# Reading one MLP weight through six access patterns in a two-layer trunk

## The chip, the cores and the metric

The kernel runs on one core of one Trainium2 chip. The metric is the device time of the program in microseconds, the median over runs. The engines are named as in the profile: PE (TensorE, matmul), PEld (its loads of the stationary operand), DVE (VectorE), ACT (ScalarE), POOL (GpSimd) and SP (SyncE, which issues the DMAs).

## The reference

A trunk of two layers over 256 tokens of width 2048, in float32. The first layer's mixer is a gated linear recurrence (HGRN2), the second one's is gated linear attention (GLA). Each mixer is followed by an MLP with a squared ReLU, and each of these four parts has a norm before it, a norm behind it and a residual add:

```python
def sqrelu_mlp(h, w_up, w_down):
    u = jax.nn.relu(h @ w_up)
    return (u * u) @ w_down

    for i in range(DEPTH):
        hn = rmsnorm(h, norm_mix_pre[i])
        m = ...    # hgrn2_mixer(hn, ...) for i = 0, gla_mixer(hn, ...) for i = 1
        h = h + rmsnorm(m, norm_mix_post[i])
        f = sqrelu_mlp(rmsnorm(h, norm_mlp_pre[i]), mlp_w_up[i], mlp_w_down[i])
        h = h + rmsnorm(f, norm_mlp_post[i])
```

`mlp_w_up[i]` is 2048 x 8192, `mlp_w_down[i]` is 8192 x 2048. The change concerns `mlp_w_down[0]`.

## The kernel before

All weights are read once, in chunks of 1 MB, 128 partitions x 2048 float32. `load_chunk` (L90) takes one of three `raw` buffers and issues the DMA on SP. `split` (L97) makes two reduced-precision parts out of each half of a chunk, 128 x 1024: `hi` by a copy on ACT (L101) and `lo` as the difference on DVE (L102), into five buffers each. The activations are held in two parts in the same way (class `Xhl`), transposed, with the contracted dimension on the partitions. A product is then three matmuls instead of one full-precision one: hi x hi, hi x lo and lo x hi.

Two forms of product follow. `gemm` (L120) has a token tile (128 tokens) of the activations as the stationary operand and 512 weight columns as the moving one; its chunks hold 4 k-tiles of 128 rows with 512 columns each, laid out by `_rows` on the host. `mm_half` (L110) issues the matmuls of half a chunk for one token tile: two k-tiles, three matmuls each (L116, L117, L118). `gemmT` (L129) has 128 weight columns as the stationary operand and the tokens as the moving one (L136 with 512 columns, both parts; L137 with 256).

The MLP goes over its 8192 hidden features in 8 groups of 1024. `up(g)` computes a group's features with 8 `gemmT` calls (in group 0 the first four column tiles come from the stage before), and `down(g)` multiplies them by the group's 1024 rows of the second weight, in 4 column blocks of 512. The running sums are kept in SBUF and added to on DVE (L443). The order is `up(0)`, then `up(g)` and `down(g - 1)` for g = 1 to 7, then `down(7)` with three column blocks; the last column block of group 7 belongs to `transition`, which also does the norms and the start of the next part. `transition` has a hand-written order; elsewhere a scheduler sets the order on each engine from the code and its buffers.

The scores of the mixers (`scores`) are products in full float32, 128 columns for each head. For `s` in `LEVELS` the moving operand is read through a pattern of its own, `comb(1, s)`: runs of `s` elements, in turn from two places 1024 + s elements apart, and so on along the tile. The products before and after the loop read contiguously.

## Time and profile before

| | |
|---|---|
| median time (two runs) | 2360.14 us (2359.75 to 2360.53) |
| span of the profiled execution, first to last instruction | 2358.0 us |
| mean granted TensorE clock | 0.997 |
| PE busy | 2328.4 us, 99% |
| DVE busy | 1499.1 us, 64% |
| ACT busy | 1193.5 us, 51% |
| DMA | 433.61 MB, 184 GB/s over the span |
| matmuls of `mm_half` (L116 to L118) | 3 x 1856, 392 ns mean duration |
| matmuls of `gemmT` (L136, L137) | 2 x 2704, 397 and 282 ns mean duration |

The profile gives the span of its execution; the median of the timed runs, 2360.14 us, is 2.1 us above it. [...] Shares of the span are averages over stages; the change is read from the stage that it lies in, the first layer's MLP, from about 540 to 1220 us.

### The profile page before, as it was taken

How to read it: one execution, taken by the hardware profiler on the slowest of the kernel's cores; microseconds unless marked ns; L12 is line 12 of the kernel's file. 1: busy time of each engine (PE TensorE's matmuls, PEld its weight loads, DVE VectorE, ACT ScalarE, POOL GpSimd, SP SyncE). 2: the span in 40 equal slices, each digit the busy share in tenths (PEclk: the TensorE clock that was granted, in tenths of full speed). 3: DMA queues.
4: the chain of work that ended last, by engine and by line, in shares of the span. 5: the costliest groups of instructions: out<-in, count | busy, mean ns of one | idle time of the engine just before them, and what ended most of it. 6: DMA issues, size and time to landing. Idle time of an engine off the chain costs nothing.

```text
span 2358.0 us, 29704 instructions
## 1 busy us (share of the span) xinstructions
PE 2328.4 (99%) x11784; PEld 1970.0 (84%) x11784; DVE 1499.1 (64%) x2047; ACT 1193.5 (51%) x1738; POOL 46.4 (2%) x22
## 2 busy tenths in 40 slices
PE   8999999999999999999989999999999999999998
PEld 7888888878888888888878888887888888888887
DVE  6787776666565565565576667656656566566556
ACT  7454554456454454454447446554645445445443
POOL 0000000020000000000010000002000000000000
PEclk9999999999999999999999999999999999999999
DMA  8545445545555555555554645454555555555554
GB/s 315 169 158 172 166 159 176 174 157 206 185 194 188 188 194 185 192 189 188 194 168 154 213 144 171 167 184 158 202 191 194 185 193 188 189 195 183 192 196 139
DMA packets 65867, 433.61 MB, mean 184 GB/s; under 512 B 7968, under 2 KB 8352, under 8 KB 15168
## 3 DMA queue, kind: packets, MB, share of 16 engines
q1 hardware_dynamic: 65728, 431.71, 53.6%
q8 instruction: 92, 1.51, 0.3%
q14 instruction: 47, 0.39, 0.0%
HBM read 429.59 MB, written 2.10 MB: 183 GB/s over the span
## 4 chain that ended last, share of the span: by engine, by line
PE 96%; DVE 3%; ACT 0%; DMA 0%; SPq 0%; issue 0%; DVEq 0%; ACTq 0%
PE mmT L136 27%; PE mm L118 17%; PE mm L117 17%; PE mm L116 17%; PE mmT L137 14%; PE sc L502 2%; DVE h L300 2%; PE tr L171 1%; DVE xhl L184 1%; PE po L563 0%; PE po L566 0%; PE po L565 0%; DMA raw<-w_hin 0%; DVE tok L279 0%; ACT xhl L182 0%; PE pg L698 0%
## 5 line engine op out<-in xcount | busy, mean ns | idle before, releaser
L102 DVE TENSOR_TENSOR lo<-raw,hi 128x1024 fp32r<-128x1024 f32 x776 | 948.7, 1225 | 734.7 <-ACT hi L101 733.6
L101 ACT ACTIVATE hi<-raw 128x1024 fp32r<-128x1024 f32 x794 | 839.6, 1061 | 997.7 <-PE mm L118 595.4
L136 PE MATMUL mmT<-xhl,hi 128*128 128x512 f32 x2704 | 954.3, 397 | 0.1
L137 PE MATMUL mmT<-xhl,lo 128*128 128x256 f32 x2704 | 761.2, 282 | 0.8 <-DVE lo L102 0.8
L116 PE MATMUL mm<-hi,xhl 128*128 128x512 f32 x1856 | 728.3, 394 | 6.0 <-ACT hi L234 6.0
L118 PE MATMUL mm<-hi,xhl 128*128 128x512 f32 x1856 | 725.2, 391 | 7.4 <-DVE xhl L184 7.4
L117 PE MATMUL mm<-lo,xhl 128*128 128x512 f32 x1856 | 726.7, 392 | 0.5 <-DVE lo L235 0.5
L136 PEld LDWEIGHTS mmT<-xhl,hi 128*128 128x128 f32 x2704 | 507.5, 188 | 122.3 <-issue 1.0
L137 PEld LDWEIGHTS mmT<-xhl,lo 128*128 128x128 f32 x2704 | 510.8, 189 | 3.4 <-issue 1.3
L118 PEld LDWEIGHTS mm<-hi,xhl 128*128 128x128 f32 x1856 | 349.6, 188 | 82.1 <-DVE xhl L184 9.2
L116 PEld LDWEIGHTS mm<-hi,xhl 128*128 128x128 f32 x1856 | 349.4, 188 | 77.8 <-ACT hi L234 7.2
L117 PEld LDWEIGHTS mm<-lo,xhl 128*128 128x128 f32 x1856 | 349.8, 188 | 72.6 <-DVE lo L235 1.4
L102 POOL TENSOR_TENSOR lo<-raw,hi 128x1024 fp32r<-128x1024 f32 x18 | 46.2, 2574 | 1603.2 <-ACT hi L101 1592.7
L145 DVE TENSOR_TENSOR half<-mmT,half 128x256 f32<-128x256 f32 x169 | 70.5, 418 | 0.0
L443 DVE TENSOR_TENSOR tok<-tok,mm 128x512 f32<-128x512 f32 x108 | 69.0, 680 | 0.0
L144 ACT COPY half<-mmT 128x256 f32<-128x256 f32 x169 | 59.6, 353 | 0.0
L429 DVE SCALAR_TENSOR_TENSOR half<-half,rr 128x256 f32<-128x256 f32 x120 | 51.1, 425 | 4.2
L432 ACT ACTIVATE half<-half 128x256 f32<-128x256 f32 x120 | 50.3, 420 | 3.7
L433 DVE TENSOR_TENSOR xhl<-half,xhl 128x256 fp32r<-128x256 f32 x120 | 50.2, 418 | 0.0
L300 DVE SCALAR_TENSOR_TENSOR h<-tok,col,h 128x512 f32<-128x512 f32 x32 | 48.5, 1553 | 0.3
L502 PEld LDWEIGHTS sc<-qk,kc 128*128 128x128 f32 x336 | 46.2, 191 | 2.8
L431 ACT ACTIVATE xhl<-half 128x256 fp32r<-128x256 f32 x120 | 48.0, 400 | 0.0
(125 smaller groups left out, 764.3 us busy)
## 6 DMA issues: line engine op xcount, KB each, us to landing
raw<-w_up SPq DMA_DIRECT2D x128, 1024.0 KB, 4.8
raw<-w_dn SPq DMA_DIRECT2D x128, 1024.0 KB, 4.8
raw<-w_hin SPq DMA_DIRECT2D x58, 1024.0 KB, 4.8
raw<-w_gin SPq DMA_DIRECT2D x48, 1024.0 KB, 4.8
raw<-w_hout SPq DMA_DIRECT2D x16, 1024.0 KB, 4.8
raw<-w_gout SPq DMA_DIRECT2D x16, 1024.0 KB, 4.8
raw<-w_hin SPq DMA_DIRECT2D x11, 512.0 KB, 7.2
wp<-npost SPq DMA_DIRECT2D x16, 256.0 KB, 3.3
```

The lines of the kernel that those rows point to most:

```text
L101: A.activation(hi, raw, AF.Copy)
L102: (eng or V).tensor_tensor(lo, raw, hi.bitcast(F32), ALU.subtract)
L116: PE.matmul(ps, xh, hi[:, kk, :], start=(k == 0), stop=False)
L117: PE.matmul(ps, xh, lo[:, kk, :], start=False, stop=False)
L118: PE.matmul(ps, xl, hi[:, kk, :], start=False, stop=(k == nk - 1))
L136: PE.matmul(ps, hi[:, kk * P:(kk + 1) * P], X.both(k), start=(k == 0), stop=False)
L137: PE.matmul(ps[:, 0, :], lo[:, kk * P:(kk + 1) * P], X.both(k)[:, 0, :], start=False, stop=(k == KT - 1))
L144: A.copy(u, ps[:, 1, :])
L145: V.tensor_tensor(u, ps[:, 0, :], u, ALU.add)
L300: V.scalar_tensor_tensor(hs, self.mw[n, t], self.r[t], hs, ALU.mult, ALU.add)
L443: V.tensor_tensor(m[n, t], m[n, t], ps[t], ALU.add)
L502: PE.matmul(ps[:, hd, :], l(hd * kt + k), r(hd * kt + k), start=(k == 0), stop=(k == kt - 1))
```

## The change

`ORDERS` holds an entry for each of the 8 groups of the hidden features: none for groups 0 and 7, and an offset and a list of [step, count] pairs (outermost first, in elements) for groups 1 to 6. On the host, `_ordered` permutes the columns inside each block of 512 of `mlp_w_down[0]`, for these groups and for the first three of the four column blocks: column j goes to the place that the pattern reaches as its j-th. In the kernel, `mm_half` reads the 512 columns of `hi` and `lo` through the pattern, so that the matmul gets them in the old order. The patterns are: 1, the even places and then the odd ones; 2, pairs of neighbours in turn from the lower and the upper half; 3, runs of 16 in turn from the two halves; 4, runs of 8 likewise; 5, backwards; 6, four runs of 128, the last one first. Everything else, the last column block and the second layer included, stays. The build with the new code issues the same instructions in the same order on every engine.

```diff
+ORDERS = (None,
+          (0, [[1, 2], [2, 256]]),
+          (0, [[2, 128], [256, 2], [1, 2]]),
+          (0, [[16, 16], [256, 2], [1, 16]]),
+          (0, [[8, 32], [256, 2], [1, 8]]),
+          (511, [[-1, 512]]),
+          (384, [[-128, 4], [1, 128]]),
+          None)
...
-    def mm_half(ps, half, hf, xs, t, nk):
+    def mm_half(ps, half, hf, xs, t, nk, order=None):
         hi, lo = (w.rearrange("p (k n) -> p k n", k=2) for w in half)
+
+        def cols(w):
+            if order is None:
+                return w
+            off, steps = order
+            return bass.AP(tensor=w.tensor, offset=w.offset + off,
+                           ap=[list(w.ap[0])] + [list(s) for s in steps])
+
         for kk in range(2):
             k = 2 * hf + kk
             xh, xl = xs(k, t)
-            PE.matmul(ps, xh, hi[:, kk, :], start=(k == 0), stop=False)
-            PE.matmul(ps, xh, lo[:, kk, :], start=False, stop=False)
-            PE.matmul(ps, xl, hi[:, kk, :], start=False, stop=(k == nk - 1))
+            PE.matmul(ps, xh, cols(hi[:, kk, :]), start=(k == 0), stop=False)
+            PE.matmul(ps, xh, cols(lo[:, kk, :]), start=False, stop=False)
+            PE.matmul(ps, xl, cols(hi[:, kk, :]), start=False, stop=(k == nk - 1))
...
-    def gemm(wap, base, nk, xs):
+    def gemm(wap, base, nk, xs, order=None):
...
-                    mm_half(ps[t], half, 2 * c + j, xs, t, nk)
+                    mm_half(ps[t], half, 2 * c + j, xs, t, nk, order)
...
         def down(g):
             for n in range(4 if g < NG - 1 else 3):
-                ps = gemm(w_dn, n * 16 + 2 * g, GK, uT[g])
+                ps = gemm(w_dn, n * 16 + 2 * g, GK, uT[g],
+                          ORDERS[g] if layer == 0 and n < 3 else None)
...
+def _ordered(rows):
+    rows = rows.reshape(4, 8, 2, P, 4, NB).copy()
+    for g, order in enumerate(ORDERS):
+        if order is None:
+            continue
+        off, steps = order
+        at = np.array([off])
+        for step, count in steps:
+            at = (at[:, None] + step * np.arange(count)).ravel()
+        laid = np.empty_like(rows[:3, g])
+        laid[..., at] = rows[:3, g]
+        rows[:3, g] = laid
+    return rows.reshape(-1, P, 4 * NB)
...
-        "w_dn0": _rows(inp["mlp_w_down"][0]),
+        "w_dn0": _ordered(_rows(inp["mlp_w_down"][0])),
```

## The prediction

> **What bounds the kernel now.** I read the page's table of busy time first, and then the shares of the chain that ended last.

> ```profile
> PE 2328.4 (99%) x11784; PEld 1970.0 (84%) x11784; DVE 1499.1 (64%) x2047; ACT 1193.5 (51%) x1738; POOL 46.4 (2%) x22
> PE 96%; DVE 3%; ACT 0%; DMA 0%; SPq 0%; issue 0%; DVEq 0%; ACTq 0%
> ```

> TensorE is busy in 99% of the span and is 96% of the chain. The change touches only the first layer's second MLP product, so I went there next. In the code that stage is a row of blocks, one for each group of 1024 hidden features: `up(g+1)`, then `down(g)`. The matmul lines of a timeline from 530 to 1225 us change between 136/137 (`up`) and 116/117/118 (`down`) at the borders of the blocks, and the answer on stretches gives what is in `down(1)` to `down(6)`, the six blocks that get new column orders.

> ```profile
> 692.04:735.62 43.58, 43.58 (x195) 1.00 0.56 193
> 780.83:824.41 43.58, 43.58 (x194) 1.00 0.57 193
> 869.62:913.21 43.59, 43.59 (x195) 1.00 0.57 193
> 958.42:1002.00 43.58, 43.58 (x195) 1.00 0.57 193
> 1047.21:1090.79 43.58, 43.58 (x194) 1.00 0.56 193
> 1136.00:1179.58 43.58, 43.58 (x194) 1.00 0.57 193
> ```

> The columns are the stretch, its length, TensorE's busy time and instructions, the granted clock and the DMA share. All six are alike: TensorE has no gap, the clock is 1.00. A block is 4 column blocks x 2 chunks x 2 halves x 2 k-tiles x 2 token tiles x 3 products = 192 matmuls (the two or three more in the count reach in over the border), so one takes 43.58 / 192 = 0.227 us. The timeline shows the same thing one by one.

> ```profile
> 1178.00 0.39 PE L118 MATMUL mm<-hi,xhl 128*128 128x512 f32 x1
> 1178.00 0.19 PEld L116 LDWEIGHTS mm<-hi,xhl 128*128 128x128 f32 x1
> 1178.22 0.39 PE L116 MATMUL mm<-hi,xhl 128*128 128x512 f32 x1
> 1178.23 0.19 PEld L117 LDWEIGHTS mm<-lo,xhl 128*128 128x128 f32 x1
> 1178.45 0.39 PE L117 MATMUL mm<-lo,xhl 128*128 128x512 f32 x1
> ```

> A matmul is recorded as 0.39 us, but the next starts 0.22 to 0.23 us later: matmuls overlap, and what counts is from start to start. The load of the next operand (0.19 us) lies beside the matmul before it. So what sets the pace is the stream of 512 columns, 0.227 / 512 = 0.443 ns for each.

> The other engines are ahead of TensorE here. One `down` block's weights, and who waits for whom from 692 to 1180 us:

> ```profile
> L101 ACT ACTIVATE hi<-raw x16: 1061/1061/1062, 692.1 to 733.1; 128x1024 fp32r<-128x1024 f32 x16
> L102 DVE TENSOR_TENSOR lo<-raw,hi x16: 1225/1226/1227, 693.2 to 734.2; 128x1024 fp32r<-128x1024 f32 x16
> DMA to landing us min/median/max: 4.7/4.9/4.9
> ACT hi L101 <- PE mm L118: 154.2, 96, 1.7
> ```

> Each half chunk is split in 1.06 us on ScalarE and 1.23 us on VectorE, while its 12 matmuls take 2.72 us; a whole chunk lands in 4.9 us and is worked off in 5.45. ScalarE waits for TensorE to give back a buffer (154.2 us in all), not the other way. A slower matmul would lengthen that wait and uncover nothing else; a longer stream would be paid in full, since no gap of TensorE is there to take it in.

> **The change part by part.** *The host reorders columns.* That is outside the timed program. Chunks keep their 1 MB, and DMA, ScalarE's copy and VectorE's subtraction go over a chunk position by position in the same shapes. The instructions of the five engines keep their order and number. Cost: nothing, as long as the load and the split stay as they are.

> *The matmuls read the columns through another pattern.* 6 groups x 3 column blocks x 48 = 864 matmuls, 144 for each order; 864 x 0.227 = 196 us of the span. Output, stationary operand and element count are unchanged. The only new cost is what the pattern does to the stream. All the reduced-precision matmuls of before read their columns in one contiguous piece, so the trace does not show it for them. But the decayed scores (L502) read their moving operand in pieces, in full f32: level s of (1, 2, 4, ... 64) takes runs of s elements in turn from two places about 4 KB apart. These are pieces of the chain of waits for the first group of heads, in order of time; the first is level 1, and the last two read contiguously.

> ```profile
> 95.05 1.33 PE sc L502 x8
> 103.54 0.97 PE sc L502 x8
> 110.52 0.89 PE sc L502 x8
> 118.35 0.89 PE sc L502 x8
> 124.80 0.89 PE sc L502 x8
> 131.24 0.89 PE sc L502 x8
> 137.69 0.89 PE sc L502 x8
> 143.44 0.89 PE sc L502 x8
> 144.33 0.89 PE po L563 x8
> ```

> Eight instructions of 128 columns each. Contiguous: 0.89 / 8 = 111 ns, or 0.87 ns a column. Level 1: 1.33 / 8 = 166 ns, 55 ns more over 128 jumps, 0.43 ns a jump, or 1.30 ns for each element. Level 2: 0.97 / 8 = 121 ns, 10 ns more over 64 jumps, 0.156 ns a jump. From level 4 on: nothing. So a jump costs something where the stream would reach the next one soon: 0.87 ns apart it costs 0.43, 1.74 apart 0.156, 3.5 apart nothing. My reading is that memory is read in aligned groups of four elements, that a visit to a group needs some 1.3 ns, and that a stream which stays longer with each group than that hides most of it. That is a reading of three rows, not a shown fact.

> The reduced-precision stream is twice as fast (0.443 ns a column), so I go by the time between jumps, not by the run's length.

> - Order 2 (pairs, in turn from two places 1 KB apart): 256 jumps, 0.89 ns apart. Nearest row: level 1 (0.87 apart). 256 x 0.43 = 110 ns, so 337 ns a matmul; 144 x 0.110 = 15.8 us. Lower end: level 2's price, 256 x 0.156 = 40 ns, 5.8 us. Upper end: a pair never quicker than at level 2 (121 / 64 = 1.89 ns), 256 x 1.89 = 484 ns, 257 more, 37.0 us.
> - Order 1 (every other column, then the rest): no far jump, but by groups of four a visit yields two elements, so again 256 visits 0.89 ns apart: 15.8 us. Lower end 0, if going on to the neighbouring group is free as in contiguous reading; upper end as in order 2, 37.0 us.
> - Order 3 (runs of 16) and order 4 (runs of 8): jumps 7.1 and 3.5 ns apart. Levels 8 and 4 have such distances and cost nothing: 0. Upper end: level 2's 0.156 ns for 32 and 64 jumps, 0.7 and 1.4 us.
> - Order 6 (four runs of 128, last first): three jumps, at most 3 x 0.43 = 1.3 ns, 0.2 us. I take 0.
> - Order 5 (backwards, one element at a time): 128 visits like contiguous reading if a group serves in either direction: 0. No row reads backwards. Upper end: a visit for each element as at level 1, 512 x 1.30 = 666 ns, 439 more, 63.2 us.

> A gain is excluded: nothing is left out, and contiguous reading has the fewest visits.

> Sum: 15.8 + 15.8 = 31.6 us. Against the profiled execution's span, 2358.0 + 31.6 = 2389.6; the median of before, 2360.14, lies 2.1 us above that span (the profile gives no other time for its execution), so 2392 us, 1.3% over before.

> [...]

> **The rivals.**

> *Nothing is paid.* The pieces are absorbed by reading ahead: a stream of 512 columns may fetch further ahead than the 128-column products of the scores, and 1 KB jumps may be kinder than 4 KB ones. For it: level 2 costs only 9%, and contiguous reduced-precision reading already goes on to the next four elements each 1.77 ns at next to no price. Against it: the level 1 row, with jumps at the same time distance as order 2. Time 2360. [...]

> *Only far jumps pay.* Order 1 walks through neighbouring groups, which reading ahead serves; order 2 alone pays: 2360 + 15.8 = 2376.

> *Backward reading is slow (the other side of 2%).* Place: the 144 matmuls of order 5, between 1047 and 1091 us of before. If a step of -1 defeats the grouping and each element is a visit, they pay up to 63.2 us; at f32's contiguous pace, 0.87 ns a column, 512 x 0.87 = 445 ns, 218 more, 31.4 us. With the forecast's 31.6 that is 2423 to 2455. With the border at 2% of 2360, 47.2 us, it decides from 47.2 - 31.6 = 15.6 us on, 108 ns more a matmul, 335 ns in all. For it: nothing in the trace steps backwards, so nothing bears it out. Against it: with whole groups fetched, the direction should not matter.

> *Anything but contiguous falls to f32's pace.* The reduced-precision stream runs at twice the f32 pace only in one piece: 864 x 0.218 = 188 us, 2548; or only for the two orders whose step isn't +1 (1 and 5), with order 2 by jumps: 288 x 0.218 + 15.8 = 78.6 us, 2439. For it: every matmul at 0.227 us reads contiguously. Against it: f32 does not change pace at all from level 4 on.

> *The change doesn't do what it says:* the pattern could be merged back into one contiguous run. None of the six can be written as one run with step 1, so I give it no chance.

> **How the numbers follow.** The forecast, orders 1 and 2 at the price of a visit: 0.38. Nothing: 0.24. Only order 2: 0.11. Backward reading: 0.18. The f32 pace for orders 1 and 5 or for all: 0.08. Faster, as drift alone: 0.01. The predicted time is the forecast's, 2392. Its own range, with orders 1 and 2 both at 5.8 or both at 37.0 us, is 2372 to 2434. The range for 8 in 10 must take in nothing (2360) and backward reading (2455); left out are the f32 pace for all and what lies below 2359: 2359 to 2455.

> A measurement of this kernel tells about 2% from no change, 47 us, so 2407 is the border. Slower: 0.18 + 0.08 + 0.02 for the forecast's upper prices = 0.28. Within 2%: 0.71. Faster: 0.01.

> **What would show it.** In the changed kernel's timeline the `down` matmuls of group 1 and of group 2, first three column blocks, should start 0.33 to 0.34 us apart, those of groups 3 to 6 and every fourth column block 0.227 as before. The stretches of `down(1)` and `down(2)` should be 59.4 us and not 43.58, the other four 43.6. The granted clock stays 1.00, ScalarE's wait for TensorE grows in the two blocks, and no other stage moves. Group 2 slow and group 1 not would be the far-jump rival; group 5 over 0.33 us the backward one; 0.227 everywhere shows that the scores' price does not carry over to this stream. The forecast's price would be wrong, with its places right, if the two groups stand at 0.27 (level 2's price) or near 0.48. What would make the whole reading wrong is a cost in groups 3, 4 or 6, where the trace has none at the same time distance.

## The result and the profile after

The changed kernel takes 2412.68 us (median of two runs, 2412.58 to 2412.78) against 2360.14 before: 1.0224 times the time before, 95% interval 1.0208 to 1.0240, so slower by a little over 2%. The span grew from 2358.0 to 2410.4 us, by 52.4.

The busy table and the shares of the chain of the changed kernel (in its lines, 134 to 136 are 116 to 118 of before, 154 and 155 are 136 and 137):

```profile
PE 2382.6 (99%) x11784; PEld 1975.2 (82%) x11784; DVE 1499.3 (62%) x2047; ACT 1193.7 (50%) x1738; POOL 46.7 (2%) x22
PE 96%; DVE 3%; ACT 0%; DMA 0%; SPq 0%; issue 0%; DVEq 0%; ACTq 0%
```

TensorE's busy time grew by 54.2 us at the same number of instructions; DVE and ACT did not move. The stretches of `down(1)` to `down(6)`, with the columns as before (stretch, length, TensorE busy and instructions, clock, DMA share, GB/s):

```profile
690.90:767.12 76.22, 76.22 (x194) 1.00 0.32 111
812.33:871.22 58.89, 58.89 (x194) 1.00 0.42 143
916.44:961.90 45.46, 45.46 (x194) 1.00 0.55 185
1007.11:1053.08 45.97, 45.97 (x194) 1.00 0.54 183
1098.29:1142.78 44.49, 44.49 (x194) 1.00 0.57 189
1188.00:1231.58 43.58, 43.58 (x194) 1.00 0.56 193
```

Each was 43.58. The excess is 32.64 + 15.31 + 1.88 + 2.39 + 0.91 + 0 = 53.1 us. The stage before ended 1.1 us earlier this time, which leaves 52.0 of the span's 52.4 us. With the fourth column block at 0.227 us, (length - 48 x 0.227) / 144 gives one matmul of orders 1 to 6: 454, 333, 240, 244, 233 and 227 ns. The timeline shows order 1 the same way, start to start 0.45 us:

```profile
694.98 0.63 PE L134 MATMUL mm<-hi,xhl 128*128 128x512 f32 x1
695.43 0.64 PE L135 MATMUL mm<-lo,xhl 128*128 128x512 f32 x1
695.89 0.63 PE L136 MATMUL mm<-hi,xhl 128*128 128x512 f32 x1
```

So order 2 costs what was forecast, order 1 twice that, and backwards almost nothing. The clock stays at 1.00 and TensorE has no gap; the copies on ACT and the subtractions on DVE take 1060 and 1225 ns on average, as before (1061 and 1225). The stream itself is slower: 454 and 333 ns a matmul with orders 1 and 2, against 227.

### The profile page after: what moved, and what is told of

Read it like the earlier page. It is cut to its first block, busy times and chain, and to the rows that moved or that the text cites. A ratio compares the mean times of both kernels' runs of the same rounds, so it can differ in the third digit from the quotient of the medians.

```text
span 2410.4 us, 29704 instructions
## 1 busy us (share of the span) xinstructions
PE 2382.6 (99%) x11784; PEld 1975.2 (82%) x11784; DVE 1499.3 (62%) x2047; ACT 1193.7 (50%) x1738; POOL 46.7 (2%) x22
## 4 chain that ended last, share of the span: by engine, by line
PE 96%; DVE 3%; ACT 0%; DMA 0%; SPq 0%; issue 0%; DVEq 0%; ACTq 0%
PE mmT L154 26%; PE mm L135 18%; PE mm L136 18%; PE mm L134 18%; PE mmT L155 13%; PE sc L521 2%; DVE h L318 2%; PE tr L189 1%; DVE xhl L202 1%; PE po L582 0%; PE po L585 0%; PE po L584 0%; DVE tok L297 0%; DMA raw<-w_hin 0%; ACT xhl L200 0%; PE pg L717 0%
## 5 line engine op out<-in xcount | busy, mean ns | idle before, releaser
L111 DVE TENSOR_TENSOR lo<-raw,hi 128x1024 fp32r<-128x1024 f32 x776 | 948.6, 1225 | 776.7 <-ACT hi L110 775.4
L110 ACT ACTIVATE hi<-raw 128x1024 fp32r<-128x1024 f32 x794 | 839.5, 1060 | 1052.2 <-PE mm L136 644.8
L134 PE MATMUL mm<-hi,xhl 128*128 128x512 f32 x1856 | 747.4, 404 | 5.6 <-ACT hi L252 5.6
L136 PE MATMUL mm<-hi,xhl 128*128 128x512 f32 x1856 | 744.3, 401 | 7.4 <-DVE xhl L202 7.4
L135 PE MATMUL mm<-lo,xhl 128*128 128x512 f32 x1856 | 745.6, 402 | 0.5 <-DVE lo L253 0.5
L136 PEld LDWEIGHTS mm<-hi,xhl 128*128 128x128 f32 x1856 | 351.1, 189 | 97.8 <-issue 12.3
```

The lines of the kernel that those rows point to most:

```text
L110: A.activation(hi, raw, AF.Copy)
L111: (eng or V).tensor_tensor(lo, raw, hi.bitcast(F32), ALU.subtract)
L134: PE.matmul(ps, xh, cols(hi[:, kk, :]), start=(k == 0), stop=False)
L135: PE.matmul(ps, xh, cols(lo[:, kk, :]), start=False, stop=False)
L136: PE.matmul(ps, xl, cols(hi[:, kk, :]), start=False, stop=(k == nk - 1))
```

## The experiments

The first five of them change only the table of orders, and the host's storing follows the table. A block's length is turned into ns a matmul as above. The runs with single elements, pairs, runs of four, lanes and full f32 are one execution each; what is read from them is the length of their blocks, each at a granted clock of 1.00. Two theories stood at first. **A (neighbours):** the reduced-precision stream is quick where two neighbouring elements are taken together; a lone element takes 452 / 512 = 0.88 ns. **B (groups of four):** each visit to an aligned group of four has a price, 452 / 256 = 1.77 ns when it goes on to the next group.

### Order 1 undone

```diff
-          (0, [[1, 2], [2, 256]]),
+          None,
```

> Order 1 undone: group 1 is stored and read as before, groups 2 to 6 keep their orders. The changed kernel's matmuls of group 1 start 452 ns apart instead of 227. If that is all that order 1 costs, group 1's block is 43.6 us again and the time is 2412.7 - 144 x 0.225 = 2380 us, 0.85% over before. If something outside the matmuls (storage, loading, splitting) were part of it, group 1's block would stay above 43.6 us or the time would come out over 2380 by more than 1 us.

Measured: 2381.0 us, 1.0089 times before (1.0072 to 1.0106), 1 us from what was expected. The blocks of groups 1 and 2:

```profile
692.38:735.97 43.59, 43.59 (x195) 1.00 0.56 193
781.18:840.07 58.89, 58.89 (x194) 1.00 0.41 143
```

Group 1 is back at 43.59 and group 2 unmoved, so order 1's cost belongs to its own block, and order 2's does not depend on it. The run undoes storing and reading together; that the cost lies in the reading rests on the timeline above, where the matmuls start 0.45 us apart without a gap.

### Single elements at a constant step

```diff
+ORDERS = (None, (0, [[1, 2], [2, 256]]), (0, [[1, 4], [4, 128]]), (0, [[1, 8], [8, 64]]),
+          (0, [[1, 16], [16, 32]]), (0, [[1, 64], [64, 8]]), (0, [[1, 256], [256, 2]]), None)
```

> Single elements at a constant step: groups 1 to 6 are read with step 2, 4, 8, 16, 64 and 256 (from place 0, then from place 1, and so on). Theory A (neighbours): the stream keeps its pace only where two neighbouring elements are taken together, and a lone element takes 0.88 ns: all six groups at 452 ns a matmul, or from step 4 on up to 512 x 1.30 = 666 ns if the price of a visit (changed kernel's order 2: 333 / 256 = 1.30 ns) limits them. Theory B (groups of four): what counts is the visit to an aligned group of four, 452 / 256 = 1.77 ns when it goes on to the next group: step 2 452 ns, step 4 512 x 1.77 = 904 ns, the wider steps 904 or, if visits to distant groups are the cheaper ones, 666. Time: A 2360 + 864 x 0.225 = 2554 us, or up to 2360 + 144 x 0.225 + 720 x 0.439 = 2709; B 2360 + 32 + 720 x 0.677 = 2880.

Measured 2519.9 us. The blocks for step 2, 4, 8, 16, 64 and 256:

```profile
691.00:767.22 76.22, 76.22 (x194) 1.00 0.32 111
812.43:889.80 77.37, 77.37 (x195) 1.00 0.32 109
935.01:1008.01 73.00, 73.00 (x194) 1.00 0.34 115
1053.22:1126.51 73.29, 73.29 (x194) 1.00 0.33 115
1171.72:1252.80 81.08, 81.08 (x195) 1.00 0.30 104
1298.01:1340.02 42.01, 42.01 (x195) 1.00 0.59 200
```

454, 462, 431, 433, 487 and 216 ns. Steps 2 to 16 would fit A (lone elements at one price, no doubling from step 2 to 4 as B has it). But step 256, which reads 0, 256, 1, 257 ..., is not only free: it is quicker than contiguous reading, 216 against 227. Neither theory allows that, for lone elements or for 512 visits.

### Pairs, and runs of four, at a constant step

In short, with one entry of the table for each p and q:

```diff
+ORDERS: (0, [[2, p // 2], [p, 512 // p], [1, 2]])   for p = 4, 8, 16, 32, 64, 128
+ORDERS: (0, [[4, q // 4], [q, 512 // q], [1, 4]])   for q = 8, 16, 32, 64, 128, 256
```

> Pairs of neighbours at a constant step: groups 1 to 6 are read as pairs with step 4, 8, 16, 32, 64 and 128 (all first pairs, then the next ones). Each group of four is visited twice, for two elements, as in orders 1 and 2. Theory A (neighbours): pairs are taken together, so no group is over order 2's 333 ns, and step 4 with its short jumps may be as low as 227. Theory B (groups of four, 1.77 ns for going on to the next group): step 4 is 256 x 1.77 = 452 ns like order 1, since only the elements taken from each group differ; the wider steps between 333 and 452. Time: A 2360 + at most 864 x 0.106 = 2452 us; B 2360 + 32 + 720 x (0.106 to 0.225) = 2468 to 2554.

> Runs of four at a constant step: groups 1 to 6 are read as aligned runs of four with step 8, 16, 32, 64, 128 and 256. 128 visits a matmul as in contiguous reading, but a jump at each. Theory A (neighbours): 227 ns plus a jump's price; by orders 3 and 4 (13 ns for 32 jumps, 17 ns for 64) 0.26 to 0.4 ns a jump, 128 jumps 33 to 52 ns, so 260 to 280 ns. Theory B: a visit of 1.30 to 1.77 ns hides behind the 1.77 ns in which four elements are taken, 227 to 240 ns. If the distance matters, the six groups differ from one another; if only the number of jumps does, they are alike. Time: A 2360 + 864 x 0.033 to 0.053 = 2389 to 2406; B 2360 to 2371.

Measured: 2558.94 us with pairs, 2379.86 with runs of four. First the blocks of pairs with step 4, 8, 16, 32, 64 and 128, then by themselves those of runs of four with step 16 and 64, the quickest and the slowest:

```profile
693.30:769.53 76.23, 76.23 (x195) 1.00 0.32 111
814.74:892.09 77.35, 77.35 (x194) 1.00 0.31 109
937.30:1010.27 72.97, 72.97 (x194) 1.00 0.33 115
1055.48:1131.67 76.19, 76.19 (x195) 1.00 0.32 111
1176.88:1257.95 81.07, 81.07 (x194) 1.00 0.30 104
1303.16:1377.95 74.79, 74.79 (x195) 1.00 0.32 112
```

```profile
781.11:824.18 43.07, 43.07 (x194) 1.00 0.56 195
961.05:1011.99 50.94, 50.94 (x195) 1.00 0.49 165
```

Pairs are no help (454, 461, 431, 453, 487 and 444 ns), which ends A. And three of them give what single elements gave at half their step: pairs with step 4 are like singles with step 2 (76.23 and 76.22), 8 like 4 (77.35 and 77.37), 16 like 8 (72.97 and 73.00). What these have in common are the elements at the even positions 0, 2, 4 ... of the order read: with pairs of step 4 these are 0, 4, 8 ..., with singles of step 2 as well. That was the hint for what follows, and no more than a hint. Pairs with step 32 and singles with step 16 have it in common too and are 453 and 433 ns; pairs with step 128 and singles with step 64 are 444 and 487. Runs of four take 231, 223, 247, 278, 268 and 250 ns for steps 8 to 256; the distance matters there, in no order that I can name.

### Two lanes

From this came **theory C**, a reading of these times: the elements at even and at odd positions of the order read are taken by two lanes side by side, and what costs is a lane's going on to another group of four. **D**, the rival: alternating between places 1 KB apart is what is quick.

```diff
+ORDERS = (None, (0, [[4, 128], [1, 2], [2, 2]]), (0, [[8, 64], [1, 4], [4, 2]]), (0, [[1, 128], [128, 4]]),
+          (0, [[1, 2], [2, 128], [256, 2]]), (0, [[1, 4], [4, 64], [256, 2]]),
+          (255, [[-1, 256], [256, 2]]), None)
```

The sixth order that ran is not the one in the expectation: it reads 255, 511, 254, 510 ..., the two halves in turn and backwards, again 64 changes a lane. The order 0, 128, 1, 129 ... is in the last experiment.

> Both earlier theories fell on step 256, which ran at 216 ns. Theory C (two lanes): in the reduced-precision stream the elements of even and of odd number are read by two lanes side by side, and what costs is that a lane goes on to another aligned group of four: up to 128 changes a lane are nearly free (contiguous 227 ns, runs of 8 and 16 240 to 243), 64 are free (step 256: 216), 256 cost 333 to 487. Theory D (two places): alternating between two places 1 KB apart is what is quick, whatever each lane does. The six groups: 1 reads 0, 2, 1, 3, 4, 6, 5, 7 ... (a lane changes 128 times): C 227 to 243, D over 430, since no two elements that follow each other are neighbours or 1 KB apart. 2 reads 0, 4, 1, 5, 2, 6, 3, 7 ... (64 changes): C 216, D over 430. 3 reads 0, 128, 256, 384, 1 ... (256 changes): C 333 to 487, D open. 4 reads 0, 256, 2, 258 ... (128 changes): C 227 to 243, D 216. 5 reads 0, 256, 4, 260 ... (256 changes): C 431 to 487, D 216. 6 reads 0, 128, 1, 129 ... in each half (64 changes): C 216, D unlike 216. Time by C: 2360 + 144 x (0.008 - 0.011 + 0.16 + 0.008 + 0.23 - 0.011) = 2415 us; by D over 2360 + 288 x 0.2 = 2418, from other groups.

Measured 2395.51 us; the six blocks:

```profile
690.85:734.43 43.58, 43.58 (x195) 1.00 0.57 193
779.64:821.62 41.98, 41.98 (x195) 1.00 0.58 200
866.82:917.10 50.28, 50.28 (x195) 1.00 0.49 167
962.30:1005.89 43.59, 43.59 (x195) 1.00 0.56 193
1051.10:1127.32 76.22, 76.22 (x194) 1.00 0.32 111
1172.53:1214.52 41.99, 41.99 (x194) 1.00 0.59 200
```

227, 216, 273, 227, 454 and 216 ns. D had over 430 for the first two and 216 for the fifth, and is out. C has five of six; the third (0, 128, 256, 384, 1 ...) is at 273, below its 333. A division of the elements by their place in memory, not by their position in the order read, is out as well: one of two such lanes would get 0, 256, 2, 258 ... both in step 256 and in order 2, and these took 216 and 333 ns.

That miss gives the rest of the account, **theory E**, an estimate fitted to these times; no view of the profile shows a lane or a group. In it a lane takes an element in 0.83 ns; a group that it must newly get takes 1.77 ns, while it may still take elements from the group before; and it keeps the last two groups, so that a return costs only the 0.83. (The 1.77 is that of theory B, from order 1; the 0.83 is what order 2 leaves for a return, 333 / 128 - 1.77.) By this count, per lane, contiguous reading has 128 new groups, 128 x 1.77 = 227. Step 256 has 64, which hide behind 256 x 0.83 = 213 (216 measured). Order 1 has 256 new: 453. Order 2 has 128 new and 128 returns, 128 x (1.77 + 0.83) = 333, and 0, 128, 256, 384 has 64 new and 192 returns, 113 + 159 = 273, both as measured. For step 64 and for pairs with step 128 a lane goes round four places; with two groups kept, each visit is then a new one, 453, and 487 and 444 were measured. Three places were not tried.

### The same in full f32

The scores' rows, from which the forecast was made, are f32. If E holds with one lane there, it must give the f32 prices too. Here the 864 matmuls of the changed blocks are done in full f32 instead of reduced precision, and the table has step 2, order 2, step 4, step 256, the order that begins 0, 2, 1, 3, and step 64.

```diff
             off, steps = order
+            w = w.bitcast(F32)
...
+            if order is not None:
+                xh, xl = xh.bitcast(F32), xl.bitcast(F32)
```

Measured 3211.8 us against 3223. The blocks of the first five:

```profile
690.94:831.46 140.52, 140.52 (x339) 1.00 0.17 60
876.67:1018.15 141.48, 141.48 (x339) 1.00 0.17 60
1063.36:1333.49 270.13, 270.13 (x339) 1.00 0.09 31
1378.70:1545.13 166.43, 166.43 (x339) 1.00 0.14 51
1590.34:1724.86 134.52, 134.52 (x338) 1.00 0.17 63
```

(Length - 10.9) / 288 is one instruction: 450, 453, 900, 540 and 429 ns, where E had 453, 439, 906, 545 and 429. Order 2 is 14 ns above E. Step 64 ran at about 860 (the stretch from 1770.07 us, where it begins, to 1906.00 has 160 instructions in 135.93 us, two of them still from the stage before), near E's 906 for all new. Contiguous reading in f32 is at the same 430 (L563 of the kernel before: two instructions of 512 columns in 0.86 us). In f32 step 256 is a loss (540 ns) and step 2 nearly free (450), the reverse of the reduced-precision stream (216 and 454 against 227), as E has it with one lane there and two here. The rival with two lanes in both is out.

### Step 256 for all weights of that form, and for both forms

The kernel before is the base of both runs. In the first, the host stores every weight that is read in 512 columns in the order of step 256, and `mm_half` reads it back:

```diff
-        hi, lo = (w.rearrange("p (k n) -> p k n", k=2) for w in half)
+        hi, lo = (w.rearrange("p (k two n) -> p k n two", k=2, two=2) for w in half)
...
-    return w.reshape(K // 512, 4, P, N // NB, NB).transpose(3, 0, 2, 1, 4).reshape(-1, P, 4 * NB)
+    w = w.reshape(K // 512, 4, P, N // NB, NB // 2, 2).swapaxes(4, 5)
+    return w.transpose(3, 0, 2, 1, 4, 5).reshape(-1, P, 4 * NB)
```

> Not one of the six orders: every weight that is read in 512 columns, in all stages, is stored in the order of step 256, so that each matmul of that form reads 0, 256, 1, 257 ... The kernel before is the base, and the result is unchanged. Theory C: 64 changes a lane instead of 128, 216 ns instead of 227 for all 5568 such matmuls, 5568 x 0.011 = 61 us less, 2299 us, ratio 0.974. A chunk of 48 / 2 = 24 matmuls then takes 5.18 us, still over the 4.9 us in which one lands and the 2 x 1.23 us of VectorE, so no other engine should become the bound. Rival: loads or splits end late at the new pace; then VectorE or the DMA show in the chain of waits and the gain is under 40 us.

Measured: 2294.44 us (four runs, 2291.7 to 2297.4), 0.9725 times before (0.9711 to 0.9740). The matmul groups, by line and with mean ns of one, and the shares of the chain:

```profile
L116 PE MATMUL mm<-hi,xhl 128*128 128x512 f32 x1856 | 709.4, 383 | 5.6 <-ACT hi L234 5.4
L118 PE MATMUL mm<-hi,xhl 128*128 128x512 f32 x1856 | 706.2, 381 | 8.2 <-DVE xhl L184 8.2
PE 95%; DVE 3%; DMA 1%; ACT 1%; SPq 0%; issue 0%; DVEq 0%; ACTq 0%
```

The gain, 65 us, is C's 61 and a little more; the mean fell from 394 and 391 ns by 10 or 11, and no other engine took over. In the second run the tokens, which are the moving operand of `gemmT`, are read in the same way:

```diff
-                PE.matmul(ps, hi[:, kk * P:(kk + 1) * P], X.both(k), start=(k == 0), stop=False)
+                PE.matmul(ps, hi[:, kk * P:(kk + 1) * P],
+                          X.both(k).rearrange("p a (h t) -> p a t h", h=NT), start=(k == 0), stop=False)
...
+        uv = u.rearrange("p (h t) -> p t h", h=NT)
+        pv = ps.rearrange("p a (t h) -> p a t h", h=NT)
+        A.copy(uv, pv[:, 1])
+        V.tensor_tensor(uv, pv[:, 0], uv, ALU.add)
```

> As the kernel with all 512-column weights in the order of step 256, and besides the products with the weights as stationary operand read the tokens as 0, 128, 1, 129 ... of each part; their sums come out in that token order and are put back by the copy and the addition that fold the two parts. Theory C: 234 ns becomes 216 to 220 and 117 becomes 107 to 112 for 2704 pairs, 2704 x (0.014 to 0.028) = 38 to 76 us less again: 2223 to 2261 us. Rival: at some 5.2 us for a 1 MB chunk the loads (4.9 us to landing, and SyncE waits for a free buffer) or ScalarE and VectorE, whose folds now go through a pattern, end last and the further gain stays under 30 us.

Measured: 2234.64 us, 0.9471 times before (0.9455 to 0.9487), 5.3% quicker than before and 7.4% quicker than the changed kernel. It is 59.8 us below the run with one form, inside the 38 to 76 expected. Its busy table:

```profile
PE 2202.1 (99%) x11784; PEld 1963.7 (88%) x11784; DVE 1532.4 (69%) x2047; ACT 1231.6 (55%) x1738; POOL 46.5 (2%) x22
```

From its timeline, the second form:

```profile
640.01 0.38 PE L136 MATMUL mmT<-xhl,hi 128*128 128x512 f32 x1
640.23 0.27 PE L138 MATMUL mmT<-xhl,lo 128*128 128x256 f32 x1
640.34 0.38 PE L136 MATMUL mmT<-xhl,hi 128*128 128x512 f32 x1
```

A pair starts every 0.33 us; in the kernel before, the starts of L136 lay 0.35 us apart on average. The folds got slower by it, as the page's groups (busy, mean ns) show:

```profile
L149 DVE TENSOR_TENSOR half<-mmT,half 128x256 f32<-128x256 f32 x169 | 103.5, 613 | 0.0
L148 ACT COPY half<-mmT 128x256 f32<-128x256 f32 x169 | 103.0, 611 | 0.0
```

They were 418 and 353 ns. That went into the idle time of DVE and ACT, and TensorE stays at 99%.

## Why the prediction was right or wrong

- **The bound, and full exposure:** right. The whole cost is TensorE's stream in the six blocks; nothing hid it and nothing else became late (53.1 us more in the blocks, 52.4 in the span).
- **The time:** forecast 2392, measured 2412.7, inside 2359 to 2455, but 2.24% over before, while 0.71 was given to "within 2%". The likeliest case had the right two blocks, and the price of one of them too small.
- **Order 2:** 337 forecast, 333 measured. The agreement is luck in part. Level 1 of the scores turned out to be the right row, but by E for a reason the prediction didn't have: level 1 in its one lane and order 2 in each of two lanes have the same mix, half new groups, half returns, (1.77 + 0.83) / 2 = 1.30 ns a visit. The prediction read this average as what any visit needs.
- **Order 1, the step that failed:** "256 visits 0.89 ns apart: 15.8 us". It measured 32.6. The price of level 1 was taken for that of any visit, but by E it is an average with returns that cost 0.83; order 1 never returns, so each visit is a new group at 1.77, as measured (454 / 256). This term is 16.8 of the 20.9 us by which forecast and time differ (the remainder is mostly orders 3, 4 and 5). Its upper end, 37.0 us, held it, and 454 ns lies by the 0.48 us that the prediction named as a sign of a wrong price.
- **Orders 3 and 4:** 0 forecast with upper ends 0.7 and 1.4; measured 1.9 and 2.4 us. The amounts are small, but the prediction had named a cost in groups 3, 4 or 6 as what would make its whole reading wrong, and here it is: a jump costs 0.26 to 0.41 ns (17 ns for 64, 13 for 32) also where level 4 and level 8 showed none. Under E these orders have 128 new groups a lane, with no slack behind which a jump could hide, while level 4 and level 8 have such slack. That is argued and not shown: runs of four with step 16 jump after every run and take 223 ns. **Order 6:** 0, as forecast (227 ns).
- **Order 5, the rival for the other side:** 233 ns, 0.9 us. Against 227 the direction hardly matters; the time passed 2% through order 1, not through backward reading.
- **"A gain is excluded":** no order of the change gained, but the reason given, that contiguous reading has the fewest visits, does not exclude one. Step 256 takes 216 ns against 227, with a visit for each element; by E the count in each lane matters, not that of the whole stream.
- **Nothing is paid, and only far jumps pay:** wrong. Order 1, with no far jump, is the dearest of the six, 454 ns.
- **The fall to f32's pace:** wrong as a mechanism, though order 1 at 454 ns looks like f32's 445. Step 256, whose every element jumps, is quicker than contiguous reading, which such a fall excludes.

## What to carry to other kernels

In this reduced-precision form, look apart at the elements at even and at odd positions of the order read: by the account that fits these runs, what counts is how many new aligned groups of four each of the two needs, at an estimated 1.77 ns each. Contiguous reading needs 128 for 512 columns, at 227 ns; the least measured is 216. Storing a weight so that the matmul reads its halves in turn needs 64 and took 5% off each of these matmuls (216 against 227 ns); done in both forms, it took 5.3% off the kernel. Before a price is carried from one operand format to another, check it in that format: the pattern that wins here loses in f32 (540 against 429 ns).

## What was not expected of the hardware

- Contiguous reading is not the quickest pattern: 227 ns for 512 columns, 216 with two interleaved halves.
- Reading backwards is nearly free, 233 ns.
- Going to and fro between two places is cheaper than going on to new ones: order 2, half of whose visits are returns, took 333 ns, order 1, which never returns, 454. By E a return costs no more than an element's pace (0.83 ns). With four places in turn in a lane the times are near order 1's (487 and 444 ns).
- The two lanes and the two kept groups are inferred from times, and E's two prices were fitted on the reduced-precision blocks; the f32 run is the one that tested it ahead. No run of elements began off a multiple of its length, so that the groups are aligned is the author's estimate. Left open is how the price of a new group depends on its place: at different steps 431 to 487 ns for 256 of them, 1.68 to 1.90 each, and runs of four between 223 and 278 ns for 128. Nor does E say why pairs with step 32 and singles with step 16, whose even positions go through the same groups, differ by 20 ns.
